# Strassen's algorithm over pairs of feature blocks, and the input phase in two groups of 1024 tokens, in a hybrid decoder block

## Chip, cores and metric

The kernel runs on one core of a Trainium2 chip. The metric is the device time of one execution in microseconds (us), as the median of several.

## The reference, cut to what matters

One layer of a hybrid decoder: 16 meta tokens and 2048 frames of width 1024 are normed and multiplied with one wide matrix `w_in`; its columns feed a gated linear attention (GLA) and a latent attention (MLA), whose outputs are gated, projected, merged and added to the residual.

```python
h = jnp.concatenate([meta, x], axis=1)
u = rms_norm(h, norm_g[l])
proj = u @ w_in[l]                       # 1024 x 6608 columns
(g_q, g_k, g_v, g_lr, g_z, m_cq, m_ckv, m_kr, m_z,
 gate_gla, gate_mla) = jnp.split(proj, cuts, axis=-1)
...
o_a = gla_chunked(q, k, v, gk)           # 4 heads, dk 128, dv 256
y_a = (rms_norm(o_a, gla_norm_g[l]).reshape(B, L, GLA_VW) * jax.nn.silu(g_z)) @ gla_proj[l]
o_b = mla_attention(m_cq, m_ckv, m_kr, ...)
y_b = (o_b * jax.nn.silu(m_z)) @ mla_proj[l]
merged = jax.nn.sigmoid(gate_gla) * y_a + jax.nn.sigmoid(gate_mla) * y_b
out = rms_norm(h + merged @ w_out[l], final_norm_g)[:, N_META:]
```

## The kernel before

Every large product is made of three matmuls of float32r operands (`mm3`, L44): each operand is split into a high part, made by a copy on ACT, and a low part, the difference, on DVE or POOL; high x high, high x low and low x high are added up in PSUM.

The input phase (`phase_ab`, L149) has three parts. First the tokens: `prep_x` (L191) loads 128 tokens, norms them, transposes them on PE and keeps them split as `u_hi` and `u_lo` (L213, L214), for all 2048 tokens, in SBUF. Beside it `natural` (L216) makes the columns of which the next steps need tokens on partitions (gate rank, latents, `v`: 1488 columns in five pieces, `PIECES`, L37): 24 matmuls per 128 tokens and piece. `load_w` (L174) loads two row blocks of `w_in` at a time and splits them (L185, L186). The meta tokens run in one pass (L229).

Then come 40 feature blocks (`feature_block`, L280), each 128 columns of `w_in` against all tokens, transposed: 8 row blocks x 3 parts x 4 tiles of 512 tokens, 96 matmuls of 512 columns on line L293, into four PSUM tiles, which are copied out at the end, two by ACT (L306) and two by DVE (L304), and stored. `z` and `mz` are first multiplied by their sigmoid (`gate`, L273: three passes on ACT, L129 to L131, and a product on DVE, L277). After every 12 matmuls a block calls `tick`, which issues a step of another part: beside the 16 early blocks (`q`, `k`, `z`) the steps of `latents` (L586), beside the late ones (`gg`, `mz`, `gm`) those of `gla` (L359), up to the last three blocks (`TAIL`), beside which the next projection's first operands are loaded.

```python
            for n, (t, (kc, x, u, s0, s1)) in enumerate(order):
                nc.tensor.matmul(acc[t], x, u[:, kc, t * 512:(t + 1) * 512], start=s0, stop=s1)
                if n % 12 == 11:
                    if later and k0 + n // 12 > 0:
                        later.pop(0)()
                    if tick is not None:
                        tick()
```

A unit of `gla` is one head over 256 tokens (`unit`, L466), in steps with `yield` between them: the gate's logarithm, a scan and decayed queries and keys (DVE, ACT and POOL, L485 to L513); transposes and scores (L518 to L537, with `v_lo` on POOL, L519); then for each 128 tokens the output `o` and the state update (L551, with the state split again, L462 and L463); the norm of the output (L555 to L559, with the five lines of `rsqrt_cols`, L57 to L68); and the product with `z` (L572). Some two or three units are under way at a time.

After the input phase `GlaProj` (L753) projects the linear attention's output, `phase_c` (L820) is the latent attention, and `Output` (L1177) the rest. The order of the instructions on each engine is made when the kernel is compiled, from the program's order and its dependencies; every DMA is issued by SP.

Of the kernel before, what the change touches and what calls it, by code (L numbers as in the profile page):

```python
# [19 lines left out]
P = 128  # L20
# [14 lines left out]
TAIL = 3  # L35
STEPS = 64
PIECES = [(0, 298), (298, 298), (596, 298), (894, 298), (1192, 296)]  # L37
# [12 lines left out]
def rsqrt_cols(nc, pool, ssq, n, inv, rows=P, tag="rs"):  # L50
    """(ssq * inv + EPS) ** -0.5 for a [rows, n] tile of sums of squares."""
# [20 lines left out]
class Scratch:  # L72
    """Intermediate results in DRAM."""

    def __init__(self, pool):
# [13 lines left out]
        self.cqt = [pool.tile([P, 1024], F32, name=f"d_cqt{t}") for t in range(NT)]  # L89
        self.qr = [pool.tile([4, P, 512], F32, name=f"d_qr{t}") for t in range(NT)]  # L90
# [58 lines left out]
def phase_ab(tc, ident, x, meta, norm_g, w_in, gate_w, gate_b, gate_b_cols, gnorm_cols, S,  # L149
             before, after):  # L150
# [16 lines left out]
    xin = xl("a_x", 2)
    gp = xl("a_g", 1)

    u_hi = ut.tile([P, KC, L], F32R, name="u_hi")  # L170
    u_lo = ut.tile([P, KC, L], F32R, name="u_lo")
    um = right("a_um", 1).tile([P, KC, 3 * M], F32R, name="um")

    def load_w(pool, pieces, width, cap, step, first=0, n=KC):  # L174
        """Columns of n row blocks of w_in, as [128, n, width], split in two."""
        hi = pool.tile([P, n, cap], F32R, tag="whi", name="w_hi")
        lo = pool.tile([P, n, cap], F32R, tag="wlo", name="w_lo")
        for k0 in range(0, n, step):
            raw = pool.tile([P, step, cap], F32, tag="wraw", name="w_raw")
            ks = slice(k0, k0 + step)  # L180
            for dst, src, cols in pieces:
                nc.sync.dma_start(
                    raw[:, :, dst:dst + cols],
                    w_in[(first + k0) * P:(first + k0 + step) * P, src:src + cols].rearrange("(k p) n -> p k n", p=P))
            nc.scalar.activation(hi[:, ks, :width], raw[:, :, :width], AF.Copy)  # L185
            nc.vector.tensor_sub(lo[:, ks, :width], raw[:, :, :width], f(hi[:, ks, :width]))  # L186
        return hi, lo

    gb = gp.tile([P, D], F32, name="gb")

    def prep_x(b):  # L191
        rows = P if b < NB else M
        xt = xin.tile([P, D], F32, tag="x", name="xt")
        nc.sync.dma_start(xt[:rows], x[b * P:(b + 1) * P, :] if b < NB else meta)
        if b == 0:
            nc.sync.dma_start(gb, norm_g.partition_broadcast(P))
        jk = gp.tile([P, D], BF16, tag="jk", name="jk")
        ssq = sm.tile([P, 1], F32, tag="ssq", name="ssq")
        nc.scalar.activation(jk[:rows], xt[:rows], AF.Square, accum_out=ssq[:rows])
        rstd = rsqrt_cols(nc, sm, ssq[:rows], 1, 1.0 / D, rows)  # L200
        nc.vector.scalar_tensor_tensor(xt[:rows], xt[:rows], rstd, gb[:rows], op0=ALU.mult, op1=ALU.mult)
        for g in range(2):
            pt = ptr.tile([P, 4, P], F32, tag="pt", name="pt")
            for j in range(4):
                kc = g * 4 + j
                nc.tensor.transpose(pt[:, j, :rows], xt[:rows, kc * P:(kc + 1) * P], ident[:rows, :rows])
            ks, o = slice(g * 4, g * 4 + 4), slice(b * P, b * P + rows)
            if b < NB:
                hi, lo = u_hi[:, ks, o], u_lo[:, ks, o]
            else:  # L210
                hi, lo = um[:, ks, :M], um[:, ks, 2 * M:]
# [1145 lines left out]
```

## Time and profile before

| | before |
|---|---|
| median of 3 runs | 2677.8 us (2676.64 to 2677.96) |
| profiled execution: span, first to last instruction | 2675.7 us |
| PE busy | 2636.1 us (99%), 15351 matmuls |
| DVE busy | 1406.9 us (53%) |
| ACT busy | 1227.3 us (46%) |
| POOL busy | 238.7 us (9%) |
| DMA | 267.78 MB, 100 GB/s on average |
| mean granted clock of TensorE | 0.998 of full speed (2.4 GHz) |

The profiled execution is one of its own; what is known of its time is its span, and the three runs beside it say how long the kernel takes. PE, DVE, ACT and POOL are TensorE, VectorE, ScalarE and GpSimd, PEld is TensorE's weight load, SP the engine that issues the DMAs. Matmuls are pipelined and their ends are modelled, so the distance between the starts of two matmuls says more than their length.

### The profile page before, as it was taken

What the parts mean: (1) busy time and instruction counts of PE and PEld (TensorE: products, weight loads), DVE (VectorE), ACT (ScalarE), POOL (GpSimd) and SP (SyncE); (2) the same over time, 40 slices, a digit from 0 to 9 for tenths busy, and PEclk for the clock granted to TensorE, in tenths of its full rate; (3) what the DMA queues carried; (4) which work ended last, traced back from release to release, by engine and by line L of the source; (5) the groups of instructions that cost most, each with busy time, mean ns of one, the idle gap of its engine ahead of it and who ended that gap; (6) DMA issues with size and microseconds to landing.
All of it is one profiled execution on the core that took longest, in us unless ns stands there. A gap on an engine that the chain in (4) does not pass through costs nothing.

```text
span 2675.7 us, 42217 instructions
## 1 busy us (share of the span) xinstructions
PE 2636.1 (99%) x15351; PEld 2322.8 (87%) x15351; DVE 1406.9 (53%) x3842; ACT 1227.3 (46%) x2947; POOL 238.7 (9%) x308
## 2 busy tenths in 40 slices
PE   8999999999999999999999999999999999999998
PEld 8999988888788888888877888999999999889997
DVE  5421102243366677776524268777776666644333
ACT  4321112254443455654335467665555555644342
POOL 0000000111011111111010010000000000121110
PEclk9999999999999999999999999999999999999999
DMA  5332224333233333343446333111111100454332
GB/s 160 96 96 75 85 73 143 109 112 116 80 110 110 121 107 114 116 123 117 137 147 197 129 119 107 56 64 41 40 41 32 36 29 21 148 165 129 111 122 67
DMA packets 246609, 267.78 MB, mean 100 GB/s; under 512 B 31376, under 2 KB 184128, under 8 KB 246400
## 3 DMA queue, kind: packets, MB, share of 16 engines
q1 hardware_dynamic: 246400, 265.09, 32.0%
q8 instruction: 120, 1.97, 0.3%
q14 instruction: 89, 0.73, 0.1%
HBM read 166.60 MB, written 98.39 MB: 99 GB/s over the span
## 4 chain that ended last, share of the span: by engine, by line
PE 88%; DMA 5%; ACT 3%; DVE 2%; issue 1%; POOL 1%; SPq 0%; DVEq 0%; ACTq 0%; POOLq 0%
PE acc L293 31%; PE acc L45 6%; PE acc L47 6%; PE acc L46 6%; PE p_tp L1030 4%; PE o_acc L46 3%; PE o_acc L45 3%; PE o_acc L47 2%; PE s L978 2%; PE s L982 2%; PE s L979 2%; PE s L981 2%; PE s L980 2%; PE oacc L47 2%; PE oacc L46 2%; PE oacc L45 2%
## 5 line engine op out<-in xcount | busy, mean ns | idle before, releaser
L293 PE MATMUL acc<-u_hi,w_hi 128*128 128x512 f32 x1280 | 436.4, 401 | 0.0
L293 PE MATMUL acc<-u_lo,w_hi 128*128 128x512 f32 x1280 | 428.8, 395 | 0.0
L293 PE MATMUL acc<-u_hi,w_lo 128*128 128x512 f32 x1280 | 427.2, 394 | 0.0
L293 PEld LDWEIGHTS acc<-u_hi,w_lo 128*128 128x128 f32 x1280 | 240.7, 188 | 56.4
L293 PEld LDWEIGHTS acc<-u_lo,w_hi 128*128 128x128 f32 x1280 | 240.4, 188 | 53.2 <-issue 0.9
L293 PEld LDWEIGHTS acc<-u_hi,w_hi 128*128 128x128 f32 x1280 | 235.1, 189 | 47.2 <-issue 1.3
L45 PE MATMUL acc<-w_hi,u_hi 128*128 128x298 f32 (+1 forms) x640 | 194.2, 305 | 2.5 <-ACT w_hi L185 2.4
L47 PE MATMUL acc<-w_hi,u_lo 128*128 128x298 f32 (+1 forms) x640 | 192.5, 302 | 0.0
L46 PE MATMUL acc<-w_lo,u_hi 128*128 128x298 f32 (+1 forms) x640 | 192.2, 301 | 0.1
L997 ACT ACTIVATE row<-row,nm,sr 128x144 f32<-128x144 f32 (+15 forms) x128 | 167.3, 1307 | 37.2 <-DVE nm L996 36.9
L1033 DVE TENSOR_TENSOR p_lo<-p_tp,p_hi 128x512 fp32r<-128x512 f32 x224 | 150.3, 687 | 49.3 <-ACT p_hi L1032 46.6
L1032 ACT ACTIVATE p_hi<-p_tp 128x512 fp32r<-128x512 f32 x224 | 129.3, 594 | 98.7 <-PE p_tp L1030 98.5
L1030 PE MATMUL p_tp<-ident,row 128*128 128x128 f32 x1088 | 168.3, 273 | 0.0
L984 DVE TENSOR_SCALAR_CACHE_REDUCE row<-s 128x388 f32<-128x388 f32 (+13 forms) x224 | 130.9, 584 | 58.8 <-PE s L982 56.6
L186 DVE TENSOR_TENSOR w_lo<-w_raw,w_hi 128x256 fp32r<-128x256 f32 (+3 forms) x188 | 89.2, 494 | 131.1 <-ACT w_hi L185 115.9
L45 PE MATMUL acc<-ob_hi,wp_hi 128*128 128x256 f32 x504 | 141.6, 281 | 3.3 <-ACT wp_hi L748 2.4
L185 ACT ACTIVATE w_hi<-w_raw 128x256 fp32r<-128x256 f32 (+3 forms) x188 | 79.5, 449 | 135.8 <-PE acc L293 96.0
L1030 PEld LDWEIGHTS p_tp<-ident,row 128*128 128x128 f32 x1088 | 128.7, 140 | 14.3 <-ACT row L997 4.7
L47 PE MATMUL acc<-ob_hi,wp_lo 128*128 128x256 f32 x504 | 141.0, 280 | 0.1
L46 PE MATMUL acc<-ob_lo,wp_hi 128*128 128x256 f32 x504 | 140.9, 280 | 0.0
L978 PE MATMUL s<-kt_hi,q_hi 128*128 128x420 f32 (+16 forms) x352 | 139.2, 396 | 0.4 <-DVE mx L987 0.4
L304 DVE COPY t_st<-acc 128x512 f32<-128x512 f32 x80 | 55.2, 690 | 155.7 <-PE acc L293 155.3
(309 smaller groups left out, 6337.0 us busy)
## 6 DMA issues: line engine op xcount, KB each, us to landing
w_raw<-in_w_in SPq DMA_DIRECT2D x160, 128.0 KB
xt<-in_x SPq DMA_DIRECT2D x32, 512.0 KB
d_nat<-nat_st SPq DMA_DIRECT2D x64, 149.0 KB
d_z<-t_st SPq DMA_DIRECT2D x32, 256.0 KB
v<-d_nat SPq DMA_DIRECT2D x64, 128.0 KB
z<-d_z SPq DMA_DIRECT2D x64, 128.0 KB
d_gg<-t_st SPq DMA_DIRECT2D x32, 256.0 KB
d_y<-z SPq DMA_DIRECT2D x64, 128.0 KB
```

Source lines behind the costliest of these rows:

```text
L45: nc.tensor.matmul(out, a_hi, b_hi, start=start, stop=False)
L46: nc.tensor.matmul(out, a_hi, b_lo, start=False, stop=False)
L47: nc.tensor.matmul(out, a_lo, b_hi, start=False, stop=stop)
L185: nc.scalar.activation(hi[:, ks, :width], raw[:, :, :width], AF.Copy)
L186: nc.vector.tensor_sub(lo[:, ks, :width], raw[:, :, :width], f(hi[:, ks, :width]))
L293: nc.tensor.matmul(acc[t], x, u[:, kc, t * 512:(t + 1) * 512], start=s0, stop=s1)
L978: nc.tensor.matmul(sv, q_hi[:, js], kt_hi[:, a:b], start=True, stop=False)
L984: nc.vector.tensor_scalar(row[:, a:b], sv, 1.0, None, op0=ALU.mult, op1=ALU.max, accum_out=mx[:, i:i + 1])
L997: nc.scalar.activation(row[:, :w], row[:, :w], AF.Exp, bias=nm, scale=sr[:, 4 * t + j:4 * t + j + 1], accum_out=rl[:, j:j + 1])
L1030: nc.tensor.transpose(tp[:, i, r * P:(r + 1) * P], rws[r][:, M + k * P:M + (k + 1) * P], ident)
L1032: nc.scalar.activation(fl(p_hi), fl(tp), AF.Copy)
L1033: nc.vector.tensor_sub(fl(p_lo), fl(tp), f(fl(p_hi)))
```

## The change

Two row blocks' halves of `w_in` (512 rows each) and two blocks of 128 columns make a 2 x 2 matrix of blocks, X; the two halves of the rows and two tiles of 512 tokens make another, Y. Their product, four blocks, is made with 7 products instead of 8 (Strassen's algorithm in Winograd's form). The sums and differences of Y (`t1` to `t4`) are made once, when the tokens are normed (`place`); those of X for each pair of blocks, on POOL (`operands`), and split like the others; the sums of the products are made when PSUM is read, on DVE, and two on POOL (`pair`). A product is 4 row blocks x 3 parts = 12 matmuls of 512 columns.

As Y with its sums takes 7 or 8 tiles where `u` took 4, only 1024 tokens fit: the whole input phase, `natural` part, early pairs with `latents`, late pairs with `gla`, now runs twice, with a group of 1024 tokens each, and `w_in` is read twice. The state of the linear attention goes through DRAM between the groups. A tick comes after each product. The last pair (first group) or two pairs (second group) run without ticks; beside them the next part is prepared: the second group's first tokens and weights, or the projection.

In `gla` the output is no longer copied out of PSUM by DVE: ACT squares it in PSUM and scales it, and the reciprocal root is taken once for a unit's two blocks. `v` is loaded later, and some buffers are fewer. The staging buffers of `GlaProj` go from 4 to 2. In `latents` the second group leaves out what depends on weights alone.

```diff
-TAIL = 3
-STEPS = 64
-PIECES = [(0, 298), (298, 298), (596, 298), (894, 298), (1192, 296)]
+WCAP = 304
+PIECES = [(0, 296), (296, 304), (600, 296), (896, 296), (1192, 296)]
...
+            c11, c21 = self.c
+            t1, t2, t3, t4 = (tmp(f"f{i}") for i in range(4))
+            split(part("y12"), pts[0])
+            nc.vector.tensor_sub(t1, pts[0], c11)
+            split(part("y22"), pts[1])
+            nc.vector.tensor_sub(t2, pts[1], t1)
+            split(part("t1"), t1)
+            nc.gpsimd.tensor_sub(t3, t2, c11)
+            nc.gpsimd.tensor_sub(t4, c21, t2)
+            split(part("t2"), t2)
+            split(part("t3"), t3, nc.gpsimd)
+            split(part("t4"), t4, nc.gpsimd)
...
+            for k in range(KC):
+                raw = self.raw.tile([P, WCAP], F32, tag="wraw", name="w_raw")
+                for dst, src, cols in pieces:
+                    nc.sync.dma_start(raw[:, dst:dst + cols], w_in[k * P:(k + 1) * P, src:src + cols])
+                split((hi[:, k, :width], lo[:, k, :width]), raw[:, :width])
...
+            order = [8 * g + i + 4 * h for i in range(4) for h in range(2)]
+            self.place(order[0])
+            self.w.append(self.load_piece(1, wb))
+            for i, b in enumerate(order):
+                if i + 1 < len(order):
+                    self.prep(order[i + 1])
+                elif g == 0:
+                    self.prep(NB)
+                for n in range(2):
+                    self.product(b, self.w[n], n)
+            for n in range(2):
+                self.meta(self.w[n], n)
+            tl.close()
+            self.xl.close()
+            self.tps.close()
+            wc = self.right("n_wc", 1)
+            for n, pool in ((2, wc), (3, self.wa), (4, wc)):
+                w = self.load_piece(n, pool)
+                for b in sorted(order):
+                    self.product(b, w, n)
+                self.meta(w, n)
...
+            for name, i, off in early + late:
+                x11, x21 = load(0, off, i)
+                x12, x22 = load(1, off, i)
+                yield parts(x11)
+                s1 = sum_("sa", nc.gpsimd.tensor_add, x21, x22)
+                yield parts(s1)
+                s2 = sum_("sb", nc.gpsimd.tensor_sub, s1, x11)
+                yield parts(s2)
+                s3 = sum_("sa", nc.gpsimd.tensor_sub, x11, x21)
+                yield parts(s3)
+                yield parts(x12)
+                yield parts(x22)
+                s4 = sum_("sa", nc.gpsimd.tensor_sub, x12, s2)
+                yield parts(s4)
...
+        def product(self, right):
+            acc = ps.tile([P, 512], F32, tag="ps", name="acc")
+            self.ahead()
+            t = self.ready.pop(0)
+            hi, lo = T[right]
+            for kc in range(KH):
+                mm3(nc, acc, t[:, 0, kc], t[:, 1, kc], hi[:, kc], lo[:, kc], kc == 0, kc == KH - 1)
+            return acc
...
+            c11 = tile_(self.up, "c11", "c11")
+            nc.scalar.activation(c11, self.product("y11"), AF.Copy)
+            step()
+            c12 = tile_(st, "st", "c12")
+            nc.scalar.activation(c12, self.product("t1"), AF.Copy)
+            step()
+            u2 = tile_(self.up, "u2", "u2")
+            nc.vector.tensor_add(u2, self.product("t2"), c11)
+            step()
+            c21 = tile_(st, "st", "c21")
+            nc.vector.tensor_add(c21, self.product("t3"), u2)
+            c22 = tile_(st, "st", "c22")
+            nc.gpsimd.tensor_add(c22, c12, c21)
+            nc.gpsimd.tensor_add(c12, c12, u2)
+            out(c22, 1, 1)
+            step()
+            nc.vector.tensor_add(c11, self.product("y21"), c11)
+            out(c11, 0, 0)
+            step()
+            nc.vector.tensor_add(c21, self.product("t4"), c21)
+            out(c21, 1, 0)
+            step()
+            nc.vector.tensor_add(c12, self.product("y22"), c12)
+            out(c12, 0, 1)
+            step()
...
+    made = None
+    nat = Natural(0)
+    for g in range(2):
+        nat.run()
+        pairs = Pairs(g)
+        nat.close()
+        pairs.open()
+        steps, close = latents_of(g)
+        count, ticks, taken, total = 40 if g == 0 else 22, 0, 0, 7 * len(early) - 3
...
+        for name, i, _ in early:
+            pairs.pair(name, i, tick)
+        pairs.drain()
+        for _ in steps:
+            pass
+        close()
+        units, close = gla(tc, ident, gate_w, gate_b, gate_b_cols, gnorm_cols, S, g)
+        tail = 1 + g
+        active, ticks, total, n = [], 0, 7 * (len(late) - tail) - 8, len(units)
+        def tick():
+            nonlocal ticks
+            ticks += 1
+            while units and (n - len(units)) * total < ticks * n:
+                active.append(units.pop(0))
+            for u in list(active):
+                if next(u, "end") == "end":
+                    active.remove(u)
+        for name, i, _ in late[:-tail]:
+            pairs.pair(name, i, tick)
+        while active or units:
+            tick()
+        close()
+        if g == 0:
+            nat = Natural(1)
         else:
+            made = after()
+        for name, i, _ in late[-tail:]:
+            pairs.pair(name, i, None)
+        pairs.drain()
+        pairs.close()
...
-    rp = right("b_r", 9)
-    w4 = right("b_w4", 4)
+    rp = right("b_r", 8)
+    w4 = right("b_w4", 2)
...
-    ms = right("b_ms", 1)
+    ms = right("b_ms", 1) if group == 0 else None
...
-        v = io1.tile([P, R, DV], F32, tag="v", name="v")
-        for j in range(R):
-            nc.sync.dma_start(v[:, j], S.nat(t * R + j)[:, N_V + h * DV:N_V + (h + 1) * DV])
-        xp = po.tile([P, W], F32, tag="o", name="xp")
+        yield
+        xp = pm.tile([P, W], F32, tag="m", name="xp")
...
-        yield
...
-        qe, ke, kp, qs = et("qe"), et("ke"), et("kp"), wt("qs")
+        qe, ke, kp, qs = et("qe"), et("ke"), et("kp"), et("qs")
...
+        for _ in range(3):
+            yield
...
-        for _ in range(4):
-            yield
-        v_hi = w4.tile([P, R, DV], F32R, tag="w", name="v_hi")
-        v_lo = w4.tile([P, R, DV], F32R, tag="w", name="v_lo")
-        nc.scalar.activation(v_hi, v, AF.Copy)
-        nc.gpsimd.tensor_sub(v_lo, v, f(v_hi))
+        v = io1.tile([P, R, DV], F32, tag="v", name="v")
+        for j in range(R):
+            nc.sync.dma_start(v[:, j], S.nat(t * R + j)[:, N_V + h * DV:N_V + (h + 1) * DV])
...
+        yield
+        v_hi = w4.tile([P, R, DV], F32R, tag="w", name="v_hi")
+        v_lo = w4.tile([P, R, DV], F32R, tag="w", name="v_lo")
+        nc.scalar.activation(v_hi, v, AF.Copy)
+        nc.gpsimd.tensor_sub(v_lo, v, f(v_hi))
...
-        for _ in range(3):
-            yield
+        yield
...
+        o = po.tile([P, R, DV], F32, tag="o", name="o")
+        ssq = sm.tile([P, R], F32, tag="ssq", name="ssq")
...
-            o = po.tile([P, DV], F32, tag="o", name="o")
-            mm3(nc, o, a_hi[:, c0], a_lo[:, c0], v_hi[:, r], v_lo[:, r], True, False)
-            mm3(nc, o, qs_hi[:, c0], qs_lo[:, c0], s_hi, s_lo, False, True)
+            mm3(nc, o[:, r], a_hi[:, c0], a_lo[:, c0], v_hi[:, r], v_lo[:, r], True, False)
+            mm3(nc, o[:, r], qs_hi[:, c0], qs_lo[:, c0], s_hi, s_lo, False, True)
...
-            ssq = sm.tile([P, 1], F32, tag="ssq", name="ssq")
-            nc.vector.tensor_copy(on[:, r], o)
...
-            nc.scalar.activation(sq, on[:, r], AF.Square, accum_out=ssq)
-            rstd = rsqrt_cols(nc, sm, ssq, 1, 1.0 / DV)
-            nc.vector.tensor_scalar(on[:, r], on[:, r], rstd, None, op0=ALU.mult)
-            yield
+            nc.scalar.activation(sq, o[:, r], AF.Square, accum_out=ssq[:, r:r + 1])
+            yield
+        rstd = rsqrt_cols(nc, sm, ssq, R, 1.0 / DV)
+        for r in range(R):
+            nc.scalar.activation(on[:, r], o[:, r], AF.Copy, scale=rstd[:, r:r + 1])
...
-        self.yr = self.right("p_yr", 4)
+        self.yr = self.right("p_yr", 2)
```

## Rows read from the trace of the kernel before

**Rows 1.** The page's part 1: busy time of each engine, its share, instructions.

```profile
PE 2636.1 (99%) x15351; PEld 2322.8 (87%) x15351; DVE 1406.9 (53%) x3842; ACT 1227.3 (46%) x2947; POOL 238.7 (9%) x308
```

**Rows 2.** Busy time by stretches; the second line names the columns.

```profile
core 0: us, PE busy (x) PEld busy (x) DVE busy (x) ACT busy (x) POOL busy (x), PEclk, DMA share, GB/s
0.00:50.00 50.00, 39.23 (x261) 37.25 (x262) 29.29 (x67) 24.90 (x53) 0.83 (x7) 1.00 0.61 172
200.00:250.00 50.00, 50.00 (x366) 49.91 (x365) 5.21 (x10) 4.65 (x10) 0.00 (x0) 1.00 0.21 66
306.00:660.00 354.00, 352.87 (x1629) 286.98 (x1628) 101.85 (x249) 116.70 (x285) 28.27 (x27) 1.00 0.37 112
720.00:1300.00 580.00, 578.62 (x2940) 480.60 (x2939) 412.55 (x1250) 288.74 (x842) 96.10 (x150) 1.00 0.37 113
1020.00:1180.00 160.00, 159.34 (x811) 133.28 (x810) 125.60 (x359) 101.59 (x274) 28.07 (x44) 1.00 0.39 117
...
1600.00:1650.00 50.00, 48.04 (x310) 41.37 (x309) 42.87 (x143) 36.47 (x107) 6.38 (x5) 1.00 0.38 114
```

**Rows 3.** Timeline of PE in a feature block with nothing beside it (start, length).

```profile
673.64 1.10 PE L293 MATMUL acc<-u_lo,w_hi 128*128 128x512 f32 x4
...
682.94 1.09 PE L293 MATMUL acc<-u_hi,w_lo 128*128 128x512 f32 x4
```

**Rows 4.** Busy time by stretches, line L293 alone (PE, PEld, clock, DMA).

```profile
720.00:1300.00 580.00, 493.76 (x1993) 363.78 (x1992) 1.00 0.37 113
```

**Rows 5.** Timeline of PE in the projection after the attention.

```profile
1519.77 0.39 PE L45 MATMUL acc<-y_hi,p_hi 128*128 128x512 f32 x1
...
1522.95 0.39 PE L47 MATMUL acc<-y_hi,p_lo 128*128 128x512 f32 x1
```

**Rows 6.** Groups of instructions by line, DVE, 720 to 1300 us.

```profile
L186 DVE TENSOR_TENSOR w_lo<-w_raw,w_hi 128x256 fp32r<-128x256 f32 x84 | 36.2, 449 | 7.6 <-ACT w_hi L185 5.0 <-PE acc L293 2.6
...
L304 DVE COPY t_st<-acc 128x512 f32<-128x512 f32 x42 | 28.9, 688 | 18.4 <-PE acc L293 18.3
...
L277 DVE TENSOR_TENSOR t_st<-t_st,e_st 128x512 f32<-128x512 f32 x34 | 26.7, 785 | 6.4 <-ACT e_st L131 6.2
L555 DVE COPY on<-o 128x256 f32<-128x256 f32 x62 | 26.1, 421 | 34.5 <-PE o L47 34.4
L559 DVE TENSOR_SCALAR on<-on,rs_y 128x256 f32<-128x256 f32 x62 | 21.9, 354 | 2.1
...
L65 DVE TENSOR_TENSOR rs_t<-rs_y 128x1 f32<-128x1 f32 x62 | 17.7, 285 | 15.2 <-ACT rs_y L64 15.2
...
L508 DVE TENSOR_TENSOR ke<-k,ek 128x256 f32<-128x256 f32 x32 | 13.4, 418 | 0.0
...
L68 DVE TENSOR_TENSOR rs_y<-rs_y,rs_t 128x1 f32<-128x1 f32 x62 | 9.9, 159 | 2.1
```

**Rows 7.** Timeline of DVE, early blocks of tokens.

```profile
47.70 1.28 DVE L214 TENSOR_TENSOR u_lo<-pt,u_hi 128x512 fp32r<-128x512 f32 x2
```

**Rows 8.** Groups of instructions by line, POOL, 720 to 1300 us.

```profile
L519 POOL TENSOR_TENSOR v_lo<-v,v_hi 128x512 fp32r<-128x512 f32 x30 | 40.1, 1337 | 241.8 <-ACT v_hi L518 223.3 <-ACT rs_t L63 10.1 <-ACT rs_y L64 8.4
L509 POOL TENSOR_TENSOR qs<-qe,dec 128x256 f32<-128x256 f32 x32 | 23.1, 722 | 33.1 <-DVE qe L507 32.1 <-DMA d_y<-z 1.0
L502 POOL TENSOR_TENSOR bc<-b,mid 128x256 f32<-128x256 f32 x32 | 19.9, 623 | 170.1 <-DVE dd L493 141.1 <-DVE mid L489 29.0
```

**Rows 9.** Timeline of DVE and of POOL, 537 to 539.5 us.

```profile
537.72 1.52 DVE L186 TENSOR_TENSOR w_lo<-w_raw,w_hi 128x256 fp32r<-128x256 f32 x1
...
537.33 1.62 POOL L644 TENSOR_TENSOR qr_st<-ro,ro 128x512 f32<-128x512 f32 x1 [6.19 <-DVE ro L643]
```

**Rows 10.** Groups of instructions by line: ACT, 720 to 1300 us, and PE, whole span.

```profile
L306 ACT ACTIVATE t_st<-acc 128x512 f32<-128x512 f32 x42 | 24.8, 590 | 18.9 <-PE acc L293 18.5
L131 ACT ACTIVATE e_st<-e_st 128x512 f32<-128x512 f32 x34 | 20.9, 623 | 0.3
...
L45 PE MATMUL acc<-y_hi,p_hi 128*128 128x512 f32 x256 | 100.9, 394 | 6.0 <-ACT y_hi L775 3.5 <-ACT p_hi L748 2.5
```

More of the change, by code (lines that the diff above doesn't have):

```diff
@@ L167, in phase_ab @@
[L167 to L187, printed above, removed]
@@ L313, in phase_ab @@
-    early = [("q", i, OFF_Q) for i in range(4)] + [("k", i, OFF_K) for i in range(4)]
-    early += [("z", i, OFF_Z) for i in range(8)]
-    late = [("gg", i, OFF_GG) for i in range(8)] + [("mz", i, OFF_MZ) for i in range(8)]
-    late += [("gm", i, OFF_GM) for i in range(8)]
-    steps, close = before()
-    ticks, taken, total = 0, 0, 8 * (len(early) - 1)
-    def tick():
-        nonlocal ticks, taken
-        ticks += 1
-        while taken < STEPS * ticks // total:
-            taken += 1
-            if next(steps, "end") == "end":
-                taken = 1 << 30
@@ L328, in phase_ab @@
-    for b in early:
-        feature_block(*b, tick)
-    for _ in steps:
-        pass
-    close()
-    units, close = gla(tc, ident, gate_w, gate_b, gate_b_cols, gnorm_cols, S)
-    active, ticks, total = [], 0, 8 * (len(late) - TAIL)
-    def tick():
-        nonlocal ticks
-        ticks += 1
-        while units and (32 - len(units)) * total < ticks * 32:
-            active.insert(0, units.pop(0))
-        for u in list(active):
-            if next(u, "end") == "end":
-                active.remove(u)
@@ L346, in phase_ab, with split @@
-    for b in late[:-TAIL]:
-        feature_block(*b, tick)
-    while active or units:
-        tick()
-    close()
-    made = after()
-    for b in late[-TAIL:]:
-        feature_block(*b)
+    tp_ = left("a_t", 1)
+    st = left("a_st", 4)
+    KH = KC // 2
+    T = {n: [tp_.tile([P, KH, 512], F32R, name=f"{n}_{e}") for e in ("hi", "lo")]
+         for n in ("y11", "y21", "y22", "t1", "t2", "t3", "t4")}
+    def split(dst, src, hl=None):
+        nc.scalar.activation(dst[0], src, AF.Copy)
+        (hl or nc.vector).tensor_sub(dst[1], src, f(dst[0]))
@@ new lines, in phase_ab, with tick @@
+    made = None
[8 more added lines that the diff above has]
+        def tick():
+            nonlocal ticks, taken
+            ticks += 1
+            while taken < count * ticks // total:
+                taken += 1
+                if next(steps, "end") == "end":
+                    taken = 1 << 30
+        for name, i, _ in early:
[7 more added lines that the diff above has]
+        active, ticks, total, n = [], 0, 7 * (len(late) - tail) - 8, len(units)
+        def tick():
+            nonlocal ticks
+            ticks += 1
+            while units and (n - len(units)) * total < ticks * n:
[6 more added lines that the diff above has]
+        while active or units:
+            tick()
+        close()
+        if g == 0:
+            nat = Natural(1)
+        else:
+            made = after()
[3 more added lines that the diff above has]
+        pairs.close()
@@ L403, in gla @@
     state = [cst.tile([P, DV], F32, name=f"state{h}") for h in range(H)]
+    if group:
+        for h in range(H):
+            nc.sync.dma_start(state[h], S.state[h])
     lr_t = {}
@@ L575, in close, with latents @@
     def close():
+        if group == 0:
+            for h in range(H):
+                nc.sync.dma_start(S.state[h], state[h])
         right.close()
         pps.close()
-    return [start()] + [unit(t, h) for t in range(L // W) for h in range(H)], close
+    half = L // W // 2
+    units = [unit(t, h) for t in range(group * half, (group + 1) * half) for h in range(H)]
+    return ([start()] if group == 0 else []) + units, close
 H, NOPE, ROPE, DV, QR, CR = 8, 128, 64, 128, 256, 128
 SCALE = 1.0 / float(np.sqrt(NOPE + ROPE))
-def latents(tc, ident, w_uq, w_ukv, gq_cols, gkv, cs, sn, sr, S):
+def latents(tc, ident, w_uq, w_ukv, gq_cols, gkv, cs, sn, sr, S, group):
     nc = tc.nc
@@ L644, in rope @@
             nc.gpsimd.tensor_add(out, t1, t2)
-        for t in [None] + list(range(NT)):
+        for t in (2, 3) if group else (None, 0, 1):
             b0, nb, r = (NB, 1, M) if t is None else (4 * t, 4, P)
```

329 lines of the change are left out of this document (199 added, 130 removed).

## Prediction

> **What bounds the kernel now.** I read the page's engine table first: PE is busy 99% of the span, DVE 53%, ACT 46% [rows 1]. A share of a whole span hides stages with different limits, so next comes the busy time by stretches [rows 2]: in 306 to 660 us (early feature blocks beside the latents) DVE is busy 0.29 of the time, in 720 to 1300 us (late blocks beside the linear attention) 0.71, in its `mz` part, 1020 to 1180 us, 0.785; PE is full in all three. So PE bounds the input phase, and DVE is the engine with the least room. A modelled end makes a busy PE look fuller than it is, so I count matmuls: in a block with nothing beside it ten rows of four start 9.30 us apart from first to last, 40 matmuls, 232.5 ns each [rows 3]. In 720 to 1300 us the line of the feature matmul ran 1993 times [rows 4], 463.4 us at that spacing. The other 116.6 us are the attention's, 3.64 us for each of 32 units (a unit is a head over 256 tokens, the start counted in); PE's own gaps there are 1.4 us [rows 2]. Hence matmuls removed from this stage are time removed, while DVE keeps up.
>
> **What is removed.** Before, a pair of feature blocks over 1024 tokens takes 2 x 8 x 3 x 2 = 96 matmuls of 512 columns; after, 7 products x 4 x 3 = 84. There are 20 pairs and two groups, so 3840 become 3360: 480 x 232.5 ns = **111.6 us**. Products with natural layout, meta products, transposes, attention and latents keep their number of matmuls; 296, 304 and 298 columns add up to the same 1488. The spacing of the new ones has two bounds: 232.5 ns, and 227 ns, at which the same shape runs in the projection after the attention (14 steps from 1519.77 to 1522.95 us [rows 5]). I take 232.5, the row of the instruction that is replaced; the other would save 3360 x 5.5 ns = 18 us more. The Trainium skill, "TensorE: Matmul & The Clock Gate", section Back-to-back issue gap, gives about 131 ns for a sustained stream at 512 columns; by that the 480 would be worth only 63 us. No row here comes near it, and the measured spacing decides.
>
> **What is added beside the late blocks.** I work per product ("slot", 12 matmuls, 2.79 us of PE). Before, the stretch had 1993/12 = 166 slots, 5.2 per unit. After, 17 units start over 69 slots in the first group and 16 over 62 in the second, 4.0 per unit, so attention adds 3.64/4.0 = 0.91 us and a slot is **3.70 us of PE**.
> DVE per slot: its 412.55 us less the blocks' own lines L186, L304 and L277 (36.2 + 28.9 + 26.7 [rows 6]) leave 320.8, 10.0 us per unit. The change takes the copies and scalings of `on` off DVE (L555 26.1, L559 21.9) and one of two reciprocal roots per unit (half of 17.7 + 4 x 9.7: five lines, of which L57, L66 and L67 lie within 0.5 us of L68 [rows 6]), 76 us in all or 2.4 per unit. 7.6/4.0 = 1.9 us per slot remain. A pair brings 7 splits and 5 adds of 128x512 to DVE, 0.64 us each in a row (two took 1.28 us [rows 7]): 12 x 0.64/7 = 1.10. Together 3.0 us, 0.81 of the slot; in `mz` pairs, with four gate products more (0.37), 3.37, or 0.91.
> POOL gets 4 sums and 2 adds per pair at 1.34 us (L519), with 2.68 us per unit (L519, L509, L502 [rows 8]): 1.15 + 0.67 = 1.82 us per slot, busy 0.49. That hurts DVE: a `w_lo` that takes 0.42 us when free (the form of L508 [rows 6]) took 1.52, until just after POOL's `qr_st` had ended [rows 9]. Both read two tiles in SBUF. Per slot DVE has 1 + 7/4.0 = 2.75 such instructions (3.3 with gates); the adds read PSUM, and I count them as free of it. Lower bound of this cost: L186 averages 449 against 418 ns, 0.03 us, while POOL's three lines are busy 83 of 580 us, 0.14; scaled to 0.49 that is 0.105 us each, 0.29 us per slot (0.35). Upper bound: each meets POOL with chance 0.49 and waits 0.6 us, half of an instruction: 0.81 (0.97). I take the lower, since it is measured on the same instruction. DVE then needs 3.29 us (3.72 in `mz`) of 3.70.
> What that costs PE: the trace has DVE at 0.785 with PE full, and at 0.86 in 1600 to 1650 us with PE losing 2 of 50 us [rows 2]. Nothing shows it fuller. At a share of 0.86 a slot lasts 3.29/0.86 = 3.83 us, 0.13 more, and 4.33 in `mz`, 0.63 more. With 91 and 56 slots: 12 + 35 = **47 us lost**. Bounds: nothing (the operands are made three products ahead, and three pairs run with no attention beside them), and with the upper cost at 0.86, 4.43 and 5.05 us, 66 + 76 = 142 us. Late next are then the `lo` halves: operands of products, `a_lo`, `s_lo`, `kt_lo`, and PE waits with all that is queued behind.
> ACT is at 0.50 in this stretch [rows 2]. It gains the first halves of 7 splits, 2 copies and two scalings per unit, some 0.6 us each (L306 [rows 10]): about 0.5 us a slot. It reaches some 3.3 of 3.70 us in `mz` slots (12 gate passes of 0.62 us, L131): a thin cover.
>
> **The rest.** Beside early pairs DVE's 0.29 of a slot of 3.2 us grows by some 0.8 us, to 0.55: hidden by PE. The t-sums of the tokens add, per two blocks of natural products (96 matmuls at 50/366 us and the transposes, some 15 us [rows 2]), 2.8 us of DVE, 3.6 of ACT and 5.3 of POOL, beside engines that idle over half: hidden. w_in is read twice: 1.05 MB a pair in 26 us for 0.52 in 28, +21 GB/s on 113, where the first stretch shows 172 [rows 2]; SP issues a piece of weights in eight loads instead of four. The `v` loads (two per unit) move on SP behind those of `q` and `k` to one slot, 3.7 us, before `v_hi` needs them; I cost that at nothing: if one lands late, ACT waits in front of `v_hi` with the next operand's first half behind it, and that one has three products of time. State out and in: four stores and four loads beside products, nothing.
> Seams: the start now happens twice. The first 50 us hold 261 instructions where 366 fit [rows 2], 14 us. In the second group normed tokens and first weights are made beside the tail pair, only the second piece's weights (their buffer frees with the last product) and its splits are open: 0 to 14, taken 5. Pieces loaded into single buffers: 0 to 6, taken 3. First operands of a group: 0 to 3, taken 1, twice. The projection after it starts with two tail pairs (39 us) as cover for three blocks before (67), and two staging buffers for four; before it lost 6.0 us waiting for its operands [rows 10]: 0 to 7 more, taken 5. Sum **15 us** (0 to 30).
>
> **Sum.** The profiled execution has a span of 2675.7 us; the median of the runs is 2677.8, 2.1 more, which I put on at the end. 2675.7 - 111.6 + 47 + 15 + 2.1 = **2628 us**.
>
> **Rivals.** (a) DVE stays covered: its waits on POOL are rare, PE stays full. No 47: 2581; with 227 ns, 2563. For it: in 720 to 1300 us PE waited for almost nothing with DVE at 0.71. Against: 0.89 and 1.0 after the change. (b) Slower: DVE and POOL exclude each other at the upper bound, DVE sets the pace of the late slots, loss 142: 2677.8 - 111.6 + 142 + 15 = 2723. It decides from 97 us of loss on, 0.66 us a slot, which is a DVE need of some 3.75 us a slot at 0.86. For it: the 1.52 us row. Against: 160 loads of that line average close to the free time. The Trainium skill, "SBUF — State Buffer", section Who interferes with whom, has this as a rule: with two SBUF inputs against a POOL instruction that reads SBUF, the second blocks fully until the first ends; the row agrees, how often they meet no page says. That the change saves no matmuls is excluded by its loops.
>
> **How the numbers follow.** Forecast 0.55 (2600 to 2668), rival (a) 0.22 (under 2600), rival (b) 0.17 (over 2683), 0.06 between. A measurement tells 0.2%, 5.4 us, from no change. Range 2572 to 2700: it leaves out the end of (a) with the faster spacing and the worse half of (b). Faster 0.77, same 0.06, slower 0.17.
>
> **What would show it.** 3360 matmuls of the new product line, 232 ns apart where nothing runs beside them; late stretches in two parts, DVE at 0.85 or more there, PE losing about 0.1 us a slot beside `gg` and `gm` and 0.6 beside `mz`; splits of 128x512 that average well over 0.69 us. Wrong if PE is full there (rival a), if split times double (rival b), or if the seams cost more than 30 us.

## The result and the profile after

The changed kernel takes **2723.8 us** (median of 4 runs, 2722.2 to 2727.1), the kernel before 2677.9 in the same comparison (4 runs): ratio 1.0168, 95% interval 1.0153 to 1.0182. It is 1.7% slower. The forecast was 2628, its range ended at 2700, and "slower" had a chance of 0.17. The profiled execution has a span of 2720.5 us.

The page's engine table, which answers to [rows 1]:

```profile
PE 2568.8 (94%) x14871; PEld 2254.7 (83%) x14871; DVE 1709.4 (63%) x3901; ACT 1386.0 (51%) x3185; POOL 618.0 (23%) x581
```

The 480 matmuls are gone (15351 to 14871) and PE is busy 67 us less, yet the span is 45 us longer: PE now waits. POOL has 2.6 times its former work. Busy time by stretches, columns as in [rows 2]: the first group's natural products, its early pairs, the middle of its late pairs, the second group's natural products, and the middle of its late pairs.

```profile
0.00:181.00 181.00, 164.92 (x1135) 159.26 (x1136) 79.67 (x170) 70.14 (x162) 29.43 (x26) 0.96 0.39 113
181.00:381.00 200.00, 185.53 (x851) 149.19 (x850) 112.19 (x197) 93.20 (x201) 78.83 (x64) 0.98 0.45 136
...
404.00:688.00 284.00, 245.37 (x1213) 198.27 (x1212) 247.13 (x520) 164.77 (x430) 121.50 (x125) 0.97 0.40 123
...
736.00:912.00 176.00, 168.18 (x1130) 161.80 (x1129) 76.28 (x146) 63.36 (x146) 36.02 (x26) 0.98 0.36 108
...
1090.00:1340.00 250.00, 217.32 (x1082) 177.11 (x1080) 217.64 (x463) 151.86 (x396) 109.81 (x112) 0.95 0.41 124
```

In the late stretches PE is busy 0.86 and 0.87, where it was full before; DVE 0.87, POOL 0.43. Neither is full, so no engine's amount of work is the bound by itself. Stage by stage, from the start of each stage's first matmul in PE's timeline:

| us | natural products | early pairs | late pairs and tail | projection |
|---|---|---|---|---|
| before | 308.8 | 403.0 | 655.5 | 185.8 |
| after (both groups) | 331.3 | 375.2 | 701.7 | 189.5 |

The late stage should have shrunk and grew by 46 us. What PE waited for in 404 to 688 us (view of the waits: total us, times, longest):

```profile
PE o L44 <- ACT s_hi L640: 11.0, 5, 4.3
PE o L44 <- ACT sq L733: 9.2, 7, 3.2
PE lr_tp L603 <- DVE kt_lo L700: 6.8, 3, 3.1
PE xp L655 <- DVE am L706: 6.0, 3, 2.3
PE suf L629 <- DVE bb L124: 1.9, 2, 1.0
PE su L44 <- DVE bb L625: 1.7, 1, 1.7
```

These six are 36.6 of PE's 38.6 idle us, and all are instructions of the attention. A product's own operand is not among them.

What DVE did there, by groups of instructions (after x the count, then busy us and mean ns; `xp` is the pair of halves of an operand, `sa` and `sb` are the sums):

```profile
L169 DVE TENSOR_TENSOR xp<-w_raw,xp 128x512 fp32r<-128x512 f32 x27 | 24.1, 892 | 2.3 <-ACT xp L168 2.0
L169 DVE TENSOR_TENSOR xp<-sa,xp 128x512 fp32r<-128x512 f32 x27 | 19.1, 708 | 0.9 <-ACT xp L168 0.8
...
L689 DVE TENSOR_TENSOR qs_lo<-qs,qs_hi 128x256 fp32r<-128x256 f32 x16 | 11.8, 737 | 0.4 <-ACT qs_hi L688 0.4
L56 DVE TENSOR_SCALAR rs_a<-ssq 128x2 f32<-128x2 f32 x15 | 11.5, 769 | 0.1
L682 DVE TENSOR_TENSOR ke<-k,ek 128x256 f32<-128x256 f32 x16 | 9.9, 621 | 0.0
...
L169 DVE TENSOR_TENSOR xp<-sb,xp 128x512 fp32r<-128x512 f32 x9 | 7.9, 876 | 0.6 <-ACT xp L168 0.6
...
L461 DVE TENSOR_TENSOR c<-acc,c 128x512 f32<-128x512 f32 x9 | 6.1, 683 | 0.0
```

The add that reads PSUM (L461) takes its free 683 ns. `ke`, a two-input step of 128x256 that took 418 before (L508 in [rows 6]), takes 621, `qs_lo`, of the same form, 737, and `rs_a`, two columns wide, 769. The timeline of DVE and POOL shows why:

```profile
481.77 0.17 DVE L56 TENSOR_SCALAR rs_a<-ssq 128x2 f32<-128x2 f32 x1
...
500.34 1.15 DVE L56 TENSOR_SCALAR rs_a<-ssq 128x2 f32<-128x2 f32 x1
...
478.95 0.31 POOL L694 MEMSET am<- 128x256 f32 x1
482.67 1.30 POOL L386 TENSOR_TENSOR sa<-w_raw 128x512 f32<-128x512 f32 x1 [3.41 <-DMA z<-d_z]
...
500.17 1.29 POOL L386 TENSOR_TENSOR sa<-w_raw,sb 128x512 f32<-128x512 f32 x1 [3.04 <-DVE xp L169]
```

With POOL idle (from 479.26 to 482.67) it takes 0.17 us; started inside a sum of POOL's it lasts until 501.49, and the sum ends at 501.46.

### The profile page after: what moved, and what is told of

The parts are those of the page before. It is cut to its first block, busy times and chain, and to the rows that moved or that the text cites. A ratio compares the mean times of both kernels' runs of the same rounds, so it can differ in the third digit from the quotient of the medians.

```text
span 2720.5 us, 42252 instructions
## 1 busy us (share of the span) xinstructions
PE 2568.8 (94%) x14871; PEld 2254.7 (83%) x14871; DVE 1709.4 (63%) x3901; ACT 1386.0 (51%) x3185; POOL 618.0 (23%) x581
## 4 chain that ended last, share of the span: by engine, by line
PE 43%; DVE 6%; DMA 5%; ACT 3%; issue 2%; POOL 2%; SPq 0%; DVEq 0%; ACTq 0%; POOLq 0%
PE p_tp L1219 4%; PE acc L46 4%; PE acc L45 4%; PE acc L44 4%; PE o_acc L45 2%; PE o_acc L44 2%; PE o_acc L46 2%; PE s L1167 2%; PE s L1171 2%; PE s L1170 2%; PE s L1169 2%; PE s L1168 2%; PE oacc L46 2%; PE oacc L45 2%; PE oacc L44 2%
## 5 line engine op out<-in xcount | busy, mean ns | idle before, releaser
L44 PE MATMUL acc<-t_hi,xp 128*128 128x512 f32 x640 | 257.3, 402 | 0.0
L46 PE MATMUL acc<-t_hi,xp 128*128 128x512 f32 x640 | 253.5, 396 | 0.4 <-DVE xp L169 0.4
L45 PE MATMUL acc<-t_lo,xp 128*128 128x512 f32 x640 | 253.3, 396 | 0.0
L45 PE MATMUL acc<-w_lo,y_hi 128*128 128x296 f32 (+1 forms) x640 | 196.5, 308 | 4.8 <-DVE w_lo L169 4.5
L44 PE MATMUL acc<-w_hi,y_hi 128*128 128x296 f32 (+1 forms) x640 | 196.6, 309 | 2.8 <-ACT w_hi L168 2.2
L46 PE MATMUL acc<-w_hi,y_lo 128*128 128x296 f32 (+1 forms) x640 | 194.9, 306 | 0.0
L44 PE MATMUL acc<-y_hi,xp 128*128 128x512 f32 x480 | 193.6, 403 | 0.0
L45 PE MATMUL acc<-y_lo,xp 128*128 128x512 f32 x480 | 191.0, 398 | 0.0
L46 PE MATMUL acc<-y_hi,xp 128*128 128x512 f32 x480 | 190.7, 397 | 0.0
L386 POOL TENSOR_TENSOR sa<-w_raw 128x512 f32<-128x512 f32 x80 | 107.9, 1348 | 352.4 <-DMA w_raw<-in_w_in 156.0
L1186 ACT ACTIVATE row<-row,nm,sr 128x144 f32<-128x144 f32 (+15 forms) x128 | 167.3, 1307 | 36.8 <-DVE nm L1185 36.6
L46 PEld LDWEIGHTS acc<-t_hi,xp 128*128 128x128 f32 x640 | 122.1, 191 | 27.2 <-DVE xp L169 0.8
L44 PEld LDWEIGHTS acc<-t_hi,xp 128*128 128x128 f32 x640 | 122.8, 192 | 23.7 <-issue 0.5
L45 PEld LDWEIGHTS acc<-t_lo,xp 128*128 128x128 f32 x640 | 122.6, 192 | 22.8
L46 PE MATMUL acc<-ob_hi,wp_lo 128*128 128x256 f32 x504 | 141.0, 280 | 0.1
```

What stands on the lines that cost most here:

```text
L44: nc.tensor.matmul(out, a_hi, b_hi, start=start, stop=False)
L45: nc.tensor.matmul(out, a_hi, b_lo, start=False, stop=False)
L46: nc.tensor.matmul(out, a_lo, b_hi, start=False, stop=stop)
L386: op(t, a, b)
L1186: nc.scalar.activation(row[:, :w], row[:, :w], AF.Exp, bias=nm, scale=sr[:, 4 * t + j:4 * t + j + 1], accum_out=rl[:, j:j + 1])
```

## Experiments

Each ran once with a profile, beside the kernel before on the same chip (2679.0 to 2682.3 us), but for the last version, which has five rounds. In the first four, L is "POOL's sums hold DVE's steps", W "DVE has too much work", and O "neither: the attention's own course in the changed loops".

**The sums left out** (the operands are single blocks).

```diff
-                s1 = sum_("sa", nc.gpsimd.tensor_add, x21, x22)
-                yield parts(s1)
...
+                yield parts(x21)
```

> Left out: POOL's four sums of weights per pair; the blocks themselves are split in their place, so splits, matmuls, DMAs and the adds of products stay (2723.8 us with the sums). Theory L (DVE's work and its waits behind POOL's two-input instructions set the pace of the late slots): POOL falls from 1.8 to 1.05 us a slot, the DVE time lost behind it by a third to a half, DVE stays above 0.8 in the late stretches; 2665 us (2640 to 2690). Rival W (DVE's own work alone, POOL does not matter): 2715 to 2725, split times unchanged. Rival O (latency of the attention's steps, with one PSUM bank a kind and fewer steps between them, whatever DVE's load): 2710 to 2725.

Measured 2648.7 us, in L's range: the sums cost 75 us, 63 of them in the late pairs (639.1 for 701.7).

**No `lo` halves of the blocks' operands**, with as many matmuls.

```diff
-                split((t[:, 0], t[:, 1]), src)
+                nc.scalar.activation(t[:, 0], src, AF.Copy)
```

> Left out: the low halves of the weights' operands, seven DVE instructions of 128x512 a pair; the third matmul of each step takes the high half and the tokens' low half again, so PE has the same 3360 matmuls. POOL as in the changed kernel. Theory L and rival W: DVE's need falls by 0.64 us a slot and more for the waits, below what covers PE; PE full in the late stretches, 2595 to 2640 us. Rival O: 2695 to 2725, DVE share falls to 0.7 and PE waits as before on the attention's instructions.

Measured 2704.0, far above what L and W gave for it. It lies in O's range, but O had also given 2710 to 2725 for the run without sums, which took 2648.7. Busy time in 404 to 688 us:

```profile
404.00:688.00 284.00, 254.25 (x1251) 207.67 (x1251) 213.13 (x462) 166.55 (x437) 119.44 (x126) 0.95 0.41 123
```

DVE's share falls from 0.87 to 0.75, below what it had in the `mz` part before [rows 2], and PE still loses 30 us. DVE's amount of work is not the cause: W falls, and L as I then had it, with the splits as the steps that matter, does too.

**The sums on DVE.**

```diff
-                s1 = sum_("sa", nc.gpsimd.tensor_add, x21, x22)
+                s1 = sum_("sa", nc.vector.tensor_add, x21, x22)
```

(and the three others alike)

> Moved: the four sums of weights per pair from POOL to DVE. Theory L: DVE gets 0.39 us a slot more work and loses some 0.3 us a slot less behind POOL, about even: 2710 to 2745 us, DVE share in the late stretches up to 0.9, splits back near 0.69 us. Rival W: 0.39 us x 147 slots / 0.86 more, 2780 to 2800. Rival O: 2720 to 2730.

Measured 2683.6, below every range: more work on the busiest helper made the kernel 40 us faster.

**Eight plain products a pair in the changed loops** (no sums, accumulation in PSUM, `t1` standing for `y12`, which this phase doesn't keep).

```diff
+            for h in range(2):
+                acc = [ps.tile([P, 512], F32, tag="ps", name="acc") for _ in range(2)]
...
+                        self.product(acc[half], t, (("y11", "t1"), ("y21", "y22"))[k][half], k == 0, k == 1)
```

> Undone: Strassen; two groups of 1024 tokens kept. Eight plain products of 12 matmuls a pair (t1 stands in for the second half of tokens' upper rows, so its output differs), four splits, four copies, no sums, ticks after each product. 3840 feature matmuls. Theory L and rival W: DVE need some 2.1 us a slot, PE full in the late stretches, time = before (2677.8) plus what two groups cost by themselves (some 25 us) less 21 us if the spacing is 227 ns: 2683 us (2670 to 2710). Rival O: the late waits stay, 2760 to 2830.

Measured 2696.4, in the range of L and W, and O is out: PE is busy 281.2 of 284 us in 404 to 688 us. That is 17 us more than the kernel before (2679.0), although these matmuls too stand 226.7 ns apart at the end of the stage, where nothing runs beside them, in place of 232.5; by that spacing 3840 of them save 22 us, so the two groups by themselves cost some 39 us, an estimate.

So POOL's sums cost 75 us, but not as DVE work. Two ways to explain it were left: they hold DVE's short steps and with them the attention's chain (A), or the attention's own POOL steps (`bc` and `qs`, for the decayed queries and keys, and `v_lo`) stand behind them in POOL's queue (Q).

**Fills in place of the sums**, as long on POOL, but reading nothing.

```diff
-                op(t, a, b)
+                nc.gpsimd.memset(t, 0.0)
+                nc.gpsimd.memset(t, 0.0)
+                nc.gpsimd.memset(t[:, :KH // 2], 0.0)
```

> Each of POOL's operand sums is replaced by fills of the same tile (128x512, 128x512, 128x256), about as long as the sum, that read nothing; the operands made of them are then zero. Theory A (what costs is that POOL's two reading inputs hold up DVE's short steps, and with them the attention's chain): the sums' cost goes although POOL is as busy as before, about 2650 us (2640 to 2670), and DVE's time above its free durations in a late stretch falls from 53 to about 25 us. Theory Q (what costs is that POOL's own steps of the attention, bc, qs and v_lo, stand behind the sums in POOL's queue): about as the changed kernel, 2710 to 2730 us. In between: both, in proportion.

Measured 2657.5. Busy time, columns as before:

```profile
404.00:688.00 284.00, 262.86 (x1328) 214.69 (x1327) 237.13 (x546) 175.14 (x452) 126.63 (x205) 0.99 0.46 139
```

POOL is as busy as in the changed kernel (126.6 for 121.5 us), PE gets 17.5 us back in this stretch, and 66 of the 75 us are gone: theory A's range. But the fills are also shorter, 0.53, 0.53 and 0.31 us where a sum takes 1.32, so a step that is held by one waits less. The timeline of DVE, then of POOL, tells the two apart:

```profile
450.96 0.29 DVE L56 TENSOR_SCALAR rs_a<-ssq 128x2 f32<-128x2 f32 x1
451.76 0.88 DVE L64 TENSOR_TENSOR rs_t<-rs_y 128x2 f32<-128x2 f32 x1 [0.29 <-ACT rs_y L63]
452.68 0.16 DVE L65 TENSOR_TENSOR rs_t<-rs_t,rs_a 128x2 f32<-128x2 f32 x1
452.87 0.24 DVE L66 TENSOR_SCALAR rs_t<-rs_t 128x2 f32<-128x2 f32 x1
...
450.71 0.52 POOL L386 MEMSET sb<- 128x512 f32 x1
451.20 1.42 POOL L718 TENSOR_TENSOR v_lo<-v,v_hi 128x512 fp32r<-128x512 f32 x1
452.56 0.52 POOL L387 MEMSET sb<- 128x512 f32 x1
```

L65, with two inputs, takes its free 0.16 us inside a fill, and L64, with two inputs too, is held until `v_lo`, which reads, has ended at 452.62. `rs_a` and L66, with one input and two columns, last until the end of a fill (451.23 and 453.08). So for two-input steps it is POOL's reading that holds; one-input steps of two columns are held by fills as well, but briefly. DVE's time above the free durations fell from 53 to 29 us in this stretch, and 26 of the 29 lie in POOL's steps that still read.

**`o` copied out of PSUM at once.**

```diff
+            nc.scalar.activation(on[:, r], o[:, r], AF.Copy)
-            nc.scalar.activation(sq, o[:, r], AF.Square, accum_out=ssq[:, r:r + 1])
+            nc.scalar.activation(sq, on[:, r], AF.Square, accum_out=ssq[:, r:r + 1])
```

> ACT copies each attention output out of PSUM at once and takes the squares and the scaling from the copy, so that the one bank for o is free earlier. In the changed kernel TensorE waits 9 us of a late stretch of 284 for the squares before it writes the next o. Both A and Q, if that bank is a link of the chain that TensorE waits on: 2695 to 2715 us. If these waits only show where a late chain is noticed: 2718 to 2728 us.

Measured 2724.4: nothing, as forecast for the second case. With the sums on POOL, the bank behind `o <- sq` is where a late chain shows, not what makes it late.

**The attention's POOL steps on DVE**, the sums left on POOL.

```diff
-        nc.gpsimd.tensor_sub(chunks(bc), chunks(b),
+        nc.vector.tensor_sub(chunks(bc), chunks(b),
```

(`qs`, `v_lo` and the clearing of `am` alike)

> The attention's own POOL steps (bc, qs, v_lo and the clearing of am) go to DVE, the sums stay on POOL. Theory Q: the attention no longer stands behind the sums, 2660 to 2695 us. Theory A: DVE's steps are held up by the sums as before and there are 4 more of them a unit (some 1.7 us of 18): 2720 to 2745 us.

Measured 2714.0, between the two ranges and nearer A's: with nothing of the attention behind the sums any more, only 10 us come back.

**Sums on DVE and `o` copied out.**

> The sums go to DVE (2683.6 us alone) and o is copied out of PSUM at once. If the o bank is a link of the chain: 2660 to 2678 us, about as fast as the kernel before or faster. If not: 2680 to 2690 us.

Measured 2673.9, in the range of the first case: with the sums off POOL the earlier bank seems worth 10 us (2683.6 without it, one run each).

**POOL emptied, in two steps**, on top of that: first the two adds for `c22` and `c12` on DVE and the cast of `a_hi` on ACT, then the attention's POOL steps on DVE too.

```diff
-            nc.gpsimd.tensor_add(c22, c12, c21)
+            nc.vector.tensor_add(c22, c12, c21)
...
-        nc.vector.tensor_copy(a_hi, am)
+        nc.scalar.activation(a_hi, am, AF.Copy)
```

> On top of the kernel with the sums on DVE and o copied out (2673.9 us): the two adds of a pair that POOL makes for c22 and c12 go to DVE, and the cast of a_hi from DVE to ACT. Theory A (POOL's reading steps cost more by holding DVE's short ones than the same work costs on DVE): 2650 to 2668 us. Rival W (DVE, 0.92 busy in a late stretch, is now itself the bound): 2676 to 2695 us.

> The same, and the attention's own POOL steps (bc, qs, v_lo, the clearing of am) on DVE too: POOL has nearly nothing left in a late stretch. Theory A: no DVE step is held any more, 2635 to 2660 us. Rival W: DVE near 1.0 of a late stretch, 2670 to 2700 us.

Measured 2627.3 and 2608.7, both below even A's ranges. The first run's two edits, the adds and the cast, were not run apart. Busy time of the second, 404 to 600 us:

```profile
404.00:600.00 196.00, 192.09 (x998) 157.04 (x997) 191.06 (x501) 148.58 (x396) 2.36 (x8) 1.00 0.47 143
```

DVE is busy 0.975 of the time and PE 0.98. The same DVE lines there:

```profile
L169 DVE TENSOR_TENSOR xp<-w_raw,xp 128x512 fp32r<-128x512 f32 x22 | 15.1, 688 | 0.0
L169 DVE TENSOR_TENSOR xp<-sa,xp 128x512 fp32r<-128x512 f32 x21 | 14.4, 685 | 0.3 <-ACT xp L168 0.3
...
L689 DVE TENSOR_TENSOR qs_lo<-qs,qs_hi 128x256 fp32r<-128x256 f32 x13 | 5.5, 423 | 0.0
...
L682 DVE TENSOR_TENSOR ke<-k,ek 128x256 f32<-128x256 f32 x13 | 5.5, 422 | 0.0
...
L56 DVE TENSOR_SCALAR rs_a<-ssq 128x2 f32<-128x2 f32 x13 | 2.2, 168 | 0.6 <-ACT sq L734 0.2
```

Every one is at its free time: 423 for 737, 168 for 769 ns.

**No sums, and POOL empty.**

> The sums left out (the operands are single blocks; 2648.7 us) and everything else of POOL's late work on DVE. What was left of the loss there, some 60 us of the late stretches, is by theory A the holding by POOL's adds and attention steps: 2600 to 2630 us. By the rival W (DVE's amount of work) it is DVE at 0.84, and more work there makes it slower: 2650 to 2670 us.

Measured 2594.0, 6 under A's range: late pairs and tail take 588.1 us in place of 639.1. So what the run without sums still lost came with POOL's other steps. Part of it is holding: DVE's time above the free durations was 25 us in 404 to 688 us there, and none is left here. But the steps themselves also got shorter (`v_lo` takes 1.41 us on POOL in the changed kernel and 0.68 on DVE), and no run separates the two.

**A version that beats both**: the kernel with POOL empty, with the clearing of `am`, a fill, back on POOL.

> The kernel with POOL nearly empty (2608.7 us), with the clearing of am, a fill that reads nothing, back on POOL. Theory A, by the run with fills (POOL's writes hold DVE little): no loss, and DVE, 0.975 busy in a late stretch there, is relieved of 32 short steps: 2600 to 2609 us, 0.971 to 0.975 of the kernel before. If POOL's fills hold DVE as its reads do, or if POOL's answer comes later than DVE's own: 2610 to 2618 us.

Measured in five rounds: **2601.3 us** (2600.4 to 2605.3), in A's range, against 2679.2 for the kernel before, ratio **0.9711** (0.9698 to 0.9725). Natural products 328.3, early pairs 359.5, late pairs and tail 597.7, projection 191.1 us. With it Strassen's form pays, by 2.9%.

**Held time and idle time side by side**, 404 to 688 us. "Held" adds up how much longer DVE's steps took than the median of the same steps with POOL empty, where that is more than 0.04 us.

| | DVE held, us | PE idle, us | DVE busy |
|---|---|---|---|
| changed kernel | 53 | 39 | 0.87 |
| no `lo` halves | 50 | 30 | 0.75 |
| attention's POOL steps on DVE | 41 | 31 | 0.91 |
| sums on DVE | 33 | 24 | 0.88 |
| fills in place of sums | 29 | 21 | 0.83 |
| sums left out | 25 | 20 | 0.83 |
| eight plain products | 21 | 3 | 0.70 |

With seven products PE's idle time goes largely with the held time and not with DVE's share. The last row shows that holding doesn't cost by itself: with eight products a pair PE has 12 matmuls more a pair beside the same attention and DVE has less to do, and almost as much held time as without the sums is covered. Which of the two covers it no run tells.

**The width of `rs_a`.** In the kernel before the same step, one column wide, stood beside POOL's `v_lo` too (timeline of before):

```profile
823.00 0.15 DVE L57 TENSOR_SCALAR rs_a<-ssq 128x1 f32<-128x1 f32 x1 [0.20 <-ACT sq L557]
823.65 0.32 DVE L65 TENSOR_TENSOR rs_t<-rs_y 128x1 f32<-128x1 f32 x1 [0.50 <-ACT rs_y L64]
...
822.64 1.31 POOL L519 TENSOR_TENSOR v_lo<-v,v_hi 128x512 fp32r<-128x512 f32 x1 [8.92 <-ACT v_hi L518]
```

There `rs_a` takes 0.15 us inside `v_lo`; `rs_t`, with two inputs, is held until `v_lo` ends at 823.95. One run makes the tile of sums three columns wide.

```diff
-        ssq = sm.tile([P, R], F32, tag="ssq", name="ssq")
+        ssq = sm.tile([P, R + 1], F32, tag="ssq", name="ssq")
```

> The tile of sums of squares gets a third column of ones, so that the steps of the reciprocal root are 128x3 in place of 128x2; nothing else changes. In the kernel before, rs_a (128x1, one input) took 0.15 us beside POOL's v_lo; in the changed one (128x2) it takes 0.6 to 1.3 us beside POOL and 0.15 without. Theory A2 (a one-input step of DVE is held where its row has an even length): rs_a and the one-input rs_t fall to about 0.15 us beside POOL too, the two-input ones stay held, and the time falls by part of the 9 us a stretch that rs_a lost: 2705 to 2720 us. Rival N (any short step is held in this kernel, whatever its width): rs_a as before, 2720 to 2728 us. If rs_a is free and the time stays at 2720 to 2728 us, rs_a isn't on the path that TensorE waits for.

```profile
L56 DVE TENSOR_SCALAR rs_a<-ssq 128x3 f32<-128x3 f32 x15 | 12.3, 819 | 0.2 <-ACT sq L734 0.2
```

Measured 2726.0, and three columns are held as two are: A2 falls. N gave the time, but goes too far with "whatever its width": once in the changed kernel a one-input step of one column (L66) starts inside POOL's add of L458, at 731.29 us, and takes 0.16 us, 0.97 before the add ends. What the runs show is one column free, two and three held. Since the step was held as before, this run can't say whether it alone lies on TensorE's path.

## Why the prediction was wrong, point by point

**What is removed** was right in its count and too small by the spacing. A pair with nothing beside it, from its first matmul to that of the next pair (84 matmuls):

```profile
1369.36 0.39 PE L44 MATMUL acc<-y_hi,xp 128*128 128x512 f32 x1
...
1388.40 0.39 PE L44 MATMUL acc<-y_hi,xp 128*128 128x512 f32 x1
```

19.04 us, 226.7 ns each: the lower of my two spacings, so 3840 x 232.5 - 3360 x 226.7 ns = 131 us, where I had 111.6.

**Beside the late blocks** is the step that failed. With 24 late pairs at the new count and spacing the stage would have taken 655.5 - 67.0 - 11.7 = 576.8 us; it took 701.7, a loss of **125 us** for my 47. PE sat idle for 84 us of this stage (354.6 - 311.5 in 381.3 to 735.9 us, 346.4 - 305.5 in 1061.5 to 1407.9 us). In another 48 us of the late stages the granted clock was at the lower level of 1.2 GHz (mean 0.97 and 0.96), which costs up to 24, a term that I didn't have. Some 11 remain in the run without sums and with POOL empty too (588.1), where PE was idle for 2 us; I don't know their cause. Three parts of that step were wrong:
- "I take the lower, since it is measured on the same instruction": the waits behind POOL. Of the DVE lines with two inputs in SBUF, and those of the reciprocal root, 15 are in the views of both the changed kernel and the one with POOL empty; the difference of their means times the count gives 45 us in 404 to 688 us. That stretch has 63 products (27 + 27 + 9 splits), so 0.71 us a slot: close to the upper bound of 0.81, far from 0.29. Both factors were too small. I counted 2.75 such steps a slot (3.3 with gates) and left out the attention's shorter ones; these lines ran 264 times, 4.2 a slot. And each lost 0.17 us, for 0.105 in the lower bound and 0.29 in the upper one. L186 was the wrong row, since it seldom met POOL before: 7 of its 84 started inside a POOL step. The right one stood in [rows 6]: L65, a one-column step with two inputs, averaged 285 ns where its like, L68, averaged 159. It comes while the attention's own `v_lo` runs, as the timeline of before shows.
- The steps counted as free. I put the joint reciprocal root of two blocks down as a saving; at two columns its one-input `rs_a` became a step that POOL holds, 769 ns for 0.15 us before.
- The price by DVE's share. I let PE lose as soon as DVE's share passed 0.86. With POOL empty DVE runs at 0.975 and PE at 0.98 beside it; with DVE at 0.75 and POOL reading, PE was at 0.90. Which steps are late seems to count: a step of 0.17 us is held by up to 1.1 us more and the attention waits for it; PE's instructions stand in a fixed order, so the products behind the attention's wait too (36.6 of PE's 38.6 idle us stand before instructions of the attention). That is read from the waits; no run held back one chosen step. "Late next are then the `lo` halves: operands of products" was wrong too: 0.4 us over the whole run were spent on them at L46. The attention's steps, named behind them there, came nearer.

**Rival (b)** gave 2723 and the median is 2723.8, but the agreement is partly luck: its bound on the time DVE is held was about right, though by fewer steps with longer waits than measured, and its mechanism, DVE setting the pace by its need, is refuted by the runs with less and with more DVE work. The Trainium skill's page "SBUF — State Buffer", section Who interferes with whom, says that a two-input DVE step conflicts with a POOL instruction that reads SBUF and not with one that only writes it; the run with fills agrees (L65 takes 0.16 us inside a fill, L64 0.88 behind `v_lo`; 2657.5 for 2723.8 us with POOL as busy). I had the rule at hand and weighed it by the wrong row.

**Beside the early pairs** I costed nothing. They took 375.2 us where the count gives 403.0 - 44.6 - 7.8 = 350.6: 25 us. In 181 to 381 us PE waited mostly behind the latents' `qr_st`, an add of POOL's in the queue with the sums, and for `ks`:

```profile
PE r_tp L909 <- POOL qr_st L833: 7.3, 5, 3.0
PE k_tp L876 <- DVE ks L868: 3.7, 3, 1.5
PE pq L44 <- DVE ro L832: 2.7, 1, 2.7
```

With POOL free of the sums (the best version) the stage takes 359.5. "Hidden by PE" looked at DVE's share alone, and left out POOL's queue and the same holding; which of the two cost more here was not tested.

**Seams**: 15 forecast; natural products 22.5 and projection 3.7 more, 26 in all, within the bounds of 0 to 30. Sum: 2675.7 - 131 + 125 + 25 + 26 = 2721, against a span of 2720.5.

**ACT** as a thin cover (0.58 in 404 to 688 us) and the `v` loads were no problem.

## What to carry to other kernels

A helper engine's free time is not free if its reads hold another engine: before giving work to POOL beside a busy DVE, look for the short DVE steps on the chain that TensorE waits for, and take their price from a step that does meet POOL, not from an average over one that doesn't. Here it was better to give DVE all of POOL's reading work (and ACT one cast and the copy of `o`) and run DVE at 0.975 than to split the work between DVE and POOL at 0.87 and 0.43. A share of busy time told neither where the loss was nor that there was room.

## What the runs showed of the hardware that was not expected

- A DVE step with one SBUF input and a row of one element was free beside POOL (`rs_a` before, 0.15 us each of the 21 times that it started inside `v_lo`); with a row of two or three it was held until POOL's instruction ended (up to 1.27 us).
- A fill on POOL did not hold a DVE step with two SBUF inputs (L65, 0.16 us inside one), but did hold `rs_a`, with one input and two columns, until it ended (0.29 us). With sums as fills, POOL at 0.45, PE was at 0.93.
- TensorE beside a DVE at 0.975 lost 4 us of 196.
- The mean granted clock was 0.97 and 0.95 in the late stretches of the changed kernel, after pauses of PE, so part of them ran at the lower level of 1.2 GHz; with POOL empty it was 1.00 in 404 to 600 us, as before [rows 2], and 0.99 in 1060 to 1300 us.
